# Both halves of the key's low part: a score matmul over 128 rows instead of 64

## The chip, the cores and the metric

The kernel runs on one core of one Trainium2 chip. The metric is device microseconds of one execution; three runs of the kernel before gave a median of 2198.81 us (2196.29 to 2199.24). Times inside a profile are microseconds from the start of its span.

## The reference, cut to what matters

One inference step of a one-layer decoder: 2048 prompt positions behind 16 meta tokens, and 8 sample positions, 1024 channels. Queries have 8 heads of 64, keys and values 2 heads of 64; every query sees itself and the 128 positions before it.

```python
h = rmsnorm(x); p = h @ w_in          # q 8x64 | k 2x64 | v 2x64 | conv GLU a 512 | b 512
s = einsum('...qhgd,...khd->...hgqk', q, k) * HEAD_DIM ** -0.5   # scores, per KV head h, group g
s = where(valid, s + rel_bias, -inf); softmax with a sink per head; o = p @ v
c = swish(layernorm(depthwise_conv_31(a * sigmoid(b))))
x = x + concat(o, c) @ w_out
x = x + square(relu(rmsnorm(x) @ w_up)) @ w_down;  y = rmsnorm(x)
```

## The kernel before

All matmuls run in a reduced 32-bit format (`F32R`), and full precision is put together from parts: each operand is split into a high part (a cast on ScalarE) and a low part (a subtraction on VectorE), and high x high, high x low and low x high are added up in PSUM. A weight slab of 128 output channels so costs 24 matmuls (`pe_step`, line 210): 8 blocks of 128 input channels times three.

The tokens are cut into five tiles (`PT`, line 25: 384, 448, 448, 448 and 320 prompt positions). Tile 0 also carries the 16 meta tokens (400 columns) and the last tile the 8 samples (328). For each tile the program (`prog`, line 943) runs the input projection (14 slabs), attention and convolution, the output projection (8 slabs) and the feed-forward part (64 slabs). Attention and convolution of a tile run as generators in the background (`Background`, line 46): after each slab of matmuls they are given a budget of VectorE time. The last slabs of tile 0's input projection share their weights with tile 1 (`in2`). The order in which each engine issues its instructions is fixed when the program is built, by a scheduler that simulates the engines and takes the ready instruction of highest priority; on the chip every engine works through its own list in order.

The score part of attention. When the slab of K has been computed (`win_evac_scaled`, m == 8, line 440), K lies on 128 partitions: KV head 0 on 0 to 63, KV head 1 on 64 to 127. For each KV head `kv`, the high part is written to both partition halves of `kh[kv]` by two casts (lines 449, 450), and the low part, one subtraction (line 451), to the head's own half of `kl`, which the two heads share. A query head's tile `q` (lines 486 to 489) holds the high part of q in the head's own half and the low part in the other half. So `q` against `kh[kv]` over 128 rows gives high x high and low x high at once, and a second matmul over the 64 rows of the own half adds high x low. These two are lines 544 and 545 in `attn_gen`. It loops over query blocks (`BQ`: 3 blocks of 128 in tile 0, 4 of 112 in tiles 1 to 3, 4 of 80 in tile 4) and over KV heads; per block and KV head it issues one group of 8 score matmuls, for 4 query heads two each, with 240 columns for blocks of 112, 208 for blocks of 80, and 256 or 144 in tile 0. In the profile the 128-row ones read `128*112 128x240` and the 64-row ones `64*112 64x240` (rows * columns of the weights, then the moving operand). In all there are 19 blocks x 8 heads = 152 pairs, of which 24 are in tile 0.

The scores of a group go to two PSUM tiles `s`; VectorE adds the bias and takes the maximum (line 558), ScalarE exponentiates and scales, TensorE transposes (`pt`, line 577), ScalarE and VectorE split the result (`ph`, `pl`), and TensorE multiplies it with V (`st`).

What else the change touches: for tiles 1 to 4, `kk` holds the two high planes and the low plane of K (line 394), and the last 128 keys of a tile go to the next one through `khist` (lines 444 to 466). In tile 0 these are single slots of the pool `tp`, 52 slots (`NSLOT`, line 1067) that also hold the input x, the normalized input's high and low parts (16 slots a tile), the queries, the convolution's inputs and sums (`pre`, line 709) and the diagonal weights of the convolution channel that TensorE computes (`dgs`, line 826; its matmuls are `cps`). `bias_setup` (line 919) spreads the relative-position bias through DRAM (`scr`, `bias`), issued from GpSimd.

Of the kernel before, what the change touches and what calls it, by code (L numbers as in the profile page):

```python
# [8 lines left out]
F32R = mybir.dt.float32r  # L9
AF = mybir.ActivationFunctionType  # L10
ALU = mybir.AluOpType
# [21 lines left out]
TM = max(TI)  # L33
# [43 lines left out]
def trunk(tc, x_in, w_all, smalls, rel, ck, cv, sconv, y_out, kv_out, ck_out, cv_out, up_out, us_out):  # L77
    nc = tc.nc
    with ExitStack() as ctx:
# [4 lines left out]
        at = ctx.enter_context(tc.tile_pool(name="at", bufs=1))  # L84
# [19 lines left out]
        def dcost(ap, extra=0.0):  # L104
            n = 1
            for s in ap.shape[1:]:
                n *= s
            clock[0] += n / 960.0 + 0.07 + extra

        def tt(out, a, b, op):  # L110
            dcost(out)
            return nc.vector.tensor_tensor(out, a, b, op=op)  # L112
# [21 lines left out]
        def cpy(out, a):  # L134
            return nc.scalar.copy(out, a)  # L135

        def f(ap):
            return ap.bitcast(F32)

        def slot(dt=F32):  # L140
            t = tp.tile([128, TS], dt, tag="t", name="t")
            return t
# [12 lines left out]
        def mm(out, lhsT, rhs, start, stop):  # L155
            return nc.tensor.matmul(out, lhsT, rhs, start=start, stop=stop)  # L156
# [222 lines left out]
        def win_alloc(i):  # L379
            n = TI[i]  # L380
            s = st[i]
            if i == 0:
                k0 = slot(F32R)
                k1 = slot(F32R)
                kl = slot(F32R)
                vt = slot()
                s["kh"], s["kl"], s["vt"], s["ko"] = [k0[:, :n], k1[:, :n]], kl[:, :n], vt[:, :n], 0
                s["u"] = []
                for c in range(4):
                    t = slot()  # L390
                    nc.vector.memset(t[:, :CW - 1], 0.0)
                    s["u"].append(t[:, :CW - 1 + n])
            else:
                kk = at.tile([128, 3, 128 + TM], F32R, tag="kk", name="kk")
                vt = at.tile([128, 128 + TM], F32, tag="vt", name="vt")
                s["kh"], s["kl"], s["vt"], s["ko"] = [kk[:, 0], kk[:, 1]], kk[:, 2], vt[:, :], 128
                s["kk"] = kk
                u = at.tile([128, 4, CW - 1 + TM], F32, tag="u", name="u")
                s["u"] = [u[:, c, :] for c in range(4)]
            s["q"] = {}  # L400
# [14 lines left out]
        def win_evac_scaled(i, m):  # L415
            n = TI[i]
            s = st[i]
            last = i == NT - 1
            if m < 8:
                c = m // 2  # L420
                if m % 2 == 0:
                    def ev(ps):
                        sg = tmp()
                        act(sg[:, :n], ps[:, :n], AF.Sigmoid)
                        s["sg"] = sg
                else:
                    def ev(ps):
                        u = s["u"][c]
                        if i > 0:
                            cpy(u[:, :CW - 1], st[i - 1]["uh"][:, c, :])  # L430
                        tt(u[:, CW - 1:CW - 1 + n], ps[:, :n], s["sg"][:, :n], ALU.mult)
                        if "uh" not in s:
                            uh = at.tile([128, 4, CW - 1], F32, tag="uh", name="uh", bufs=2)
                            s["uh"] = uh
                        e = CW - 1 + OFF[i] + PT[i]
                        cpy(s["uh"][:, c, :], u[:, e - (CW - 1):e])
                        s.setdefault("udone", []).append(c)
                        if c == 3 and last:
                            nc.gpsimd.dma_start(up_out, s["uh"])
            elif m == 8:  # L440
                def ev(ps):
                    o = s["ko"]
                    if i > 0:
                        p = st[i - 1]["khist"]
                        cpy(s["kk"][:, :, :128], f(p))
                    for kv in range(2):
                        hr, xr = HR[kv], HR[1 - kv]
                        kh = s["kh"][kv][:, o:o + n]
                        cpy(kh[hr], ps[hr, :n])
                        cpy(kh[xr], ps[hr, :n])  # L450
                        tt(s["kl"][hr, o:o + n], ps[hr, :n], f(kh[hr]), ALU.subtract)
                    e = o + OFF[i] + PT[i]
                    if last:
                        e0 = OFF[i] + PT[i]
                        kvo = at.tile([128, 2, 128 + NSMP], F32, tag="kvo", name="kvo")
                        s["kvo"] = kvo
                        cpy(kvo[:, 0, :], ps[:, e0 - 128:e0 + NSMP])
                    else:
                        kn = at.tile([128, 3, 128], F32R, tag="khist", name="khist")
                        if i > 0:  # L460
                            cpy(kn, f(s["kk"][:, :, e - 128:e]))
                        else:
                            cpy(kn[:, 0, :], f(s["kh"][0][:, e - 128:e]))
                            cpy(kn[:, 1, :], f(s["kh"][1][:, e - 128:e]))
                            cpy(kn[:, 2, :], f(s["kl"][:, e - 128:e]))
                        s["khist"] = kn
            elif m == 9:
                def ev(ps):
                    o = s["ko"]
                    if i > 0:  # L470
                        cpy(s["vt"][:, :128], st[i - 1]["vhist"])
                    cpy(s["vt"][:, o:o + n], ps[:, :n])
                    e = o + OFF[i] + PT[i]
                    if last:
                        cpy(s["kvo"][:, 1, :], s["vt"][:, e - 128:e + NSMP])
                        nc.gpsimd.dma_start(kv_out, s["kvo"])
                    else:
                        vn = at.tile([128, 128], F32, tag="vhist", name="vhist")
                        cpy(vn, s["vt"][:, e - 128:e])
                        s["vhist"] = vn  # L480
            else:
                def ev(ps):
                    c = m - 10
                    for kv in range(2):
                        hr, xr = HR[kv], HR[1 - kv]
                        q = slot(F32R)
                        s["q"][kv * 4 + c] = q
                        act(q[hr, :n], ps[hr, :n], AF.Copy, scale=HD ** -0.5)
                        stt(q[xr, :n], ps[hr, :n], HD ** -0.5, f(q[hr, :n]), ALU.mult, ALU.subtract)
                    if last:  # L490
                        if c == 0:
                            qs = at.tile([128, NSMP, NH], F32, tag="qs", name="qs")
                            nc.vector.memset(qs, 0.0)
                            s["qs"] = qs
                        e = OFF[i] + PT[i]
                        for kv in range(2):
                            r = HR[kv]
                            act(s["qs"][r, :, kv * 4 + c], ps[r, e:e + NSMP], AF.Copy, scale=HD ** -0.5)
            return ev
# [14 lines left out]
        def attn_gen(i, blocks):  # L514
            s = st[i]
            bq = BQ[i]
            for b in blocks:
                q0 = b * bq
                qc = OFF[i] + q0
                kc = s["ko"] + qc  # L520
                k0 = max(kc - 128, 0)
                na = kc - k0
                nk = na + bq
# [11 lines left out]
                for kv in range(2):  # L535
                    hr, xr = HR[kv], HR[1 - kv]
                    sp = []
                    for c in range(4):
                        if c % 2 == 0:
                            t = pa.tile([128, 2, 256], F32, tag="s", name="s")  # L540
                            sp.append(t)
                        o = sp[-1][:bq, c % 2, :nk]
                        q = s["q"][kv * 4 + c]
                        mm(o, q[:, qc:qc + bq], s["kh"][kv][:, k0:k0 + nk], True, False)
                        mm(o, q[hr, qc:qc + bq], s["kl"][hr, k0:k0 + nk], False, True)
                    if i > 0 or NS0 == 1:
                        yield STEP
                    p = at.tile([128, 4, 256], F32, tag="p", name="p", bufs=NPB)
# [43 lines left out]
                    o = ot[:, :4 * bq]  # L592
# [575 lines left out]
def build(shapes):  # L1168
    import concourse.bacc as bacc

    nc = bacc.Bacc("TRN2", target_bir_lowering=False, num_devices=1)
    args = [nc.dram_tensor(n, s, F32, kind="ExternalInput").ap() for n, s in shapes.items()]
    args += [nc.dram_tensor(n, s, F32, kind="ExternalOutput").ap() for n, s in _OUTS]
    with tile.TileContext(nc, schedule_with_timeline_sim=True) as tc:
        trunk(tc, *args)
    return nc
# [28 lines left out]
```

## Time and profile before

| | |
|---|---|
| median of 3 runs | 2198.81 us |
| span of the profiled execution | 2192.0 us |
| median less span | 6.8 us |
| TensorE matmul busy | 2143.6 us (98%) |
| TensorE weight loads busy | 1976.0 us (90%) |
| VectorE busy | 1520.4 us (69%) |
| ScalarE busy | 1178.2 us (54%) |

The profiled execution's own time outside its span is not given, so the span stands for it. TensorE's 48.4 us without a matmul lie in four places: the first 20 us, the stretch from 50 to 97 us, short waits up to 360 us, and the last 92 us. Matmuls are pipelined: the duration of one is not the time it takes from the next, so costs of matmuls are read here from start to start.

### The profile page before, as it was taken

Reading aid. Unit: us, or ns where it says so; the run is one execution under the profiler, and the core shown is the slowest. Engines: PE = TensorE matmul, PEld = TensorE weight load, DVE = VectorE, ACT = ScalarE, POOL = GpSimd, SP = SyncE. Lnnn points to the kernel's source line nnn. Section 1 sums busy time; section 2 is a strip of 40 time slices with the busy share of each in tenths; the row PEclk is TensorE's granted clock in tenths of the full one; section 3 lists DMA queues with packets and bytes.
Section 4 is the critical chain, followed back from the end, with each engine's and each line's share of the span. In section 5 each row is a group of like instructions: output and inputs, shape, how many; then the busy total and the mean of one; then the engine's idle time right before and its main releaser. Section 6 shows DMA issues by size and latency. Waiting matters only on the chain.

```text
span 2192.0 us, 29953 instructions
## 1 busy us (share of the span) xinstructions
PE 2143.6 (98%) x11330; PEld 1976.0 (90%) x11330; DVE 1520.4 (69%) x2585; ACT 1178.2 (54%) x2151; POOL 50.0 (2%) x95
## 2 busy tenths in 40 slices
PE   7599999999999999999999999999999999999998
PEld 6587899999998898989989898899998989999998
DVE  5497698986866987647758886466787754565444
ACT  6357475467545454655445447454654464454443
POOL 1000000000000000000000000000010100000000
PEclk9799999999999999999999999999999999999999
DMA  5311323324433222225332222335432322435442
GB/s 186 68 49 54 130 91 121 116 106 139 162 132 105 98 87 97 97 98 171 140 108 94 96 96 87 106 121 183 148 106 100 126 90 103 150 117 187 145 152 103
DMA packets 77952, 255.67 MB, mean 117 GB/s; under 512 B 9805, under 2 KB 20173, under 8 KB 77808
## 3 DMA queue, kind: packets, MB, share of 16 engines
q1 hardware_dynamic: 72000, 238.08, 31.5%
q0 software_dynamic: 5088, 14.93, 2.4%
q8 instruction: 89, 1.46, 0.3%
q10 hardware_dynamic: 720, 0.76, 0.1%
q14 instruction: 55, 0.45, 0.1%
HBM read 241.97 MB, written 11.75 MB: 116 GB/s over the span
## 4 chain that ended last, share of the span: by engine, by line
PE 95%; issue 2%; DMA 2%; DVE 1%; POOL 0%; ACT 0%; DVEq 0%; POOLq 0%; ACTq 0%
PE mm L156 87%; PE s L156 4%; PE st L156 2%; DMA scr<-t 2%; PE pt L577 1%; PE cps L156 1%; DVE t L116 0%; DMA bias<-scr 0%; DMA t<-x_in 0%; DVE wlo L112 0%; PE mx L156 0%; PE st L525 0%; PE st L526 0%; DVE t L112 0%; DVE m L116 0%
## 5 line engine op out<-in xcount | busy, mean ns | idle before, releaser
L156 PE MATMUL mm<-t,whi 128*128 128x448 f32 (+3 forms) x6560 | 1354.2, 353 | 12.4 <-ACT t L131 8.7
L156 PEld LDWEIGHTS mm<-t,whi 128*128 128x128 f32 x6560 | 1168.8, 189 | 86.7 <-ACT t L131 9.5
L135 ACT CAST whi<-raw 128x1024 fp32r<-128x1024 f32 x424 | 443.7, 1049 | 599.0 <-PE mm L156 485.4
L156 PE MATMUL mm<-t,wlo 128*128 128x448 f32 (+3 forms) x3280 | 714.0, 350 | 0.0
L112 DVE TENSOR_TENSOR wlo<-raw,whi 128x1024 fp32r<-128x1024 f32 x424 | 516.7, 1219 | 262.5 <-PE mm L156 140.1
L156 PEld LDWEIGHTS mm<-t,wlo 128*128 128x128 f32 x3280 | 588.8, 188 | 34.0
L116 DVE SCALAR_TENSOR_TENSOR t<-u,sm,t 128x448 f32<-128x448 f32 (+1 forms) x480 | 300.8, 645 | 3.5
L112 DVE TENSOR_TENSOR t<-mm,t 128x448 f32<-128x448 f32 (+2 forms) x200 | 116.6, 583 | 209.7 <-PE mm L156 206.7
L112 DVE TENSOR_TENSOR t<-m,t 128x448 fp32r<-128x448 f32 (+3 forms) x234 | 133.1, 581 | 25.6 <-ACT t L135 24.9
L135 ACT CAST t<-m 128x448 fp32r<-128x448 f32 (+3 forms) x236 | 125.3, 536 | 17.5 <-DVE m L116 12.8
L131 ACT ACTIVATE m<-mm 128x448 f32<-128x448 f32 (+2 forms) x176 | 90.0, 511 | 56.8 <-PE mm L156 49.3
L131 ACT ACTIVATE m<-t 128x448 f32<-128x448 f32 (+3 forms) x140 | 72.1, 542 | 65.0 <-DVE t L112 42.1
L132 ACT ACTIVATE p<-p,nm 112x240 f32<-112x240 f32 (+3 forms) x152 | 72.2, 476 | 49.0 <-DVE nm L121 48.7
L131 ACT ACTIVATE m<-m 128x448 f32<-128x448 f32 (+3 forms) x164 | 90.1, 549 | 3.9
L558 DVE CUSTOM_DVE_ANT_0 p<-s,bias,sm 112x240 f32<-112x240 f32 (+3 forms) x152 | 61.7, 449 | 30.8 <-DMA bias<-scr 25.7
L156 PE MATMUL s<-kk,t 128*112 128x240 f32 (+3 forms) x256 | 72.4, 341 | 1.7 <-DVE t L116 1.7
L156 PEld LDWEIGHTS s<-kk,t 128*112 128x112 f32 (+3 forms) x256 | 42.2, 165 | 32.0 <-issue 8.2
L131 ACT ACTIVATE p<-p,rd 112x240 f32<-112x240 f32 (+3 forms) x152 | 62.0, 476 | 9.9 <-DVE rd L127 9.7
L112 DVE TENSOR_TENSOR ss<-ss,m 128x448 f32<-128x448 f32 (+3 forms) x100 | 58.3, 583 | 6.9 <-ACT m L131 3.6
L127 DVE RECIPROCAL rs<-m 128x448 f32<-128x448 f32 (+2 forms) x15 | 41.6, 2776 | 24.1 <-ACT m L131 24.1
L116 DVE SCALAR_TENSOR_TENSOR t<-t,sm 128x384 f32<-128x384 f32 (+1 forms) x98 | 56.6, 612 | 2.4 <-ACT t L131 2.0
L156 PE MATMUL mm<-cah,whi 128*128 128x448 f32 (+2 forms) x160 | 55.6, 349 | 1.6 <-ACT cah L135 0.7
(174 smaller groups left out, 1144.8 us busy)
## 6 DMA issues: line engine op xcount, KB each, us to landing
raw<-w_all SPq DMA_DIRECT2D x424, 512.0 KB, 3.2
t<-x_in SPq DMA_DIRECT2D x40, 224.0 KB, 5.0
y_out<-t POOLq DMA_DIRECT2D x24, 224.0 KB, 3.4
t<-x_in SPq DMA_DIRECT2D x16, 164.0 KB, 3.6
t<-x_in POOLq DMA_DIRECT2D x8, 224.0 KB, 6.3
t<-x_in SPq DMA_DIRECT2D x8, 200.0 KB, 5.1
scr<-t POOLq DMA_DIRECT2D x1, 1536.0 KB, 33.2
t<-x_in SPq DMA_DIRECT2D x8, 192.0 KB, 5.1
```

Source lines behind the costliest of these rows:

```text
L112: return nc.vector.tensor_tensor(out, a, b, op=op)
L116: return nc.vector.scalar_tensor_tensor(out, a, s, b, op0=op0, op1=op1)
L127: return nc.vector.reciprocal(out, a)
L131: return nc.scalar.activation(out, a, f, bias=bias, scale=scale)
L132: return nc.scalar.activation(out, a, f, bias=bias, scale=scale, accum_out=accum_out)
L135: return nc.scalar.copy(out, a)
L156: return nc.tensor.matmul(out, lhsT, rhs, start=start, stop=stop)
L558: nc.vector.tensor_tensor_reduce(out=p[:bq, c, :nk], in0=sp[c // 2][:bq, c % 2, :nk], in1=bias[:bq, h, b0:b0 + nk], scale=1.0, scalar=sm[: ...
L577: nc.tensor.transpose(t[:r, c * bq:(c + 1) * bq], p[:bq, c, a:a + r], idn[:bq, :bq])
```

## The change

The low part of K gets a plane of its own for each KV head, written into both partition halves, and the second score matmul then runs over all 128 rows, with the same weights `q` as the first. (Its other half now multiplies the query's low part with the key's low part, a product that was not formed before.) Per tile this adds two subtractions; `kk` and `khist` get a fourth plane; tile 0 uses one slot of `tp` more. The on-chip memory that is set aside for the descriptors of GpSimd's DMAs is halved, to 8192 bytes a partition.

```diff
@@ win_alloc @@
-                kl = slot(F32R)
+                l0 = slot(F32R)
+                l1 = slot(F32R)
...
-                kk = at.tile([128, 3, 128 + TM], F32R, tag="kk", name="kk")
+                kk = at.tile([128, 4, 128 + TM], F32R, tag="kk", name="kk")
...
@@ win_evac_scaled, m == 8 @@
-                        tt(s["kl"][hr, o:o + n], ps[hr, :n], f(kh[hr]), ALU.subtract)
+                        kl = s["kl"][kv][:, o:o + n]
+                        tt(kl[hr], ps[hr, :n], f(kh[hr]), ALU.subtract)
+                        tt(kl[xr], ps[hr, :n], f(kh[hr]), ALU.subtract)
...
-                        kn = at.tile([128, 3, 128], F32R, tag="khist", name="khist")
+                        kn = at.tile([128, 4, 128], F32R, tag="khist", name="khist")
...
@@ attn_gen @@
                         mm(o, q[:, qc:qc + bq], s["kh"][kv][:, k0:k0 + nk], True, False)
-                        mm(o, q[hr, qc:qc + bq], s["kl"][hr, k0:k0 + nk], False, True)
+                        mm(o, q[:, qc:qc + bq], s["kl"][kv][:, k0:k0 + nk], False, True)
...
@@ build @@
-    nc = bacc.Bacc("TRN2", target_bir_lowering=False, num_devices=1)
+    nc = bacc.Bacc("TRN2", target_bir_lowering=False, num_devices=1, dynamic_dma_scratch_size=8192)
```

## Rows read from the trace of the kernel before

**Rows 1.** The page: busy time of each engine, and the chain that ended last.
```profile
PE 2143.6 (98%) x11330; PEld 1976.0 (90%) x11330; DVE 1520.4 (69%) x2585; ACT 1178.2 (54%) x2151; POOL 50.0 (2%) x95
...
PE 95%; issue 2%; DMA 2%; DVE 1%; POOL 0%; ACT 0%; DVEq 0%; POOLq 0%; ACTq 0%
```

**Rows 2.** Stretches: length, busy time (instructions) of each engine, granted clock, DMA share, GB/s.
```profile
150.00:216.00 66.00, 64.92 (x282) 49.01 (x281) 53.20 (x117) 47.48 (x114) 0.00 (x0) 1.00 0.11 40
...
251.00:690.00 439.00, 436.98 (x2376) 415.62 (x2376) 340.58 (x564) 249.93 (x455) 4.30 (x8) 1.00 0.35 122
690.00:1148.00 458.00, 458.00 (x2249) 413.20 (x2247) 324.93 (x527) 241.63 (x426) 4.32 (x8) 1.00 0.32 111
```

**Rows 3.** Groups by shape: count, busy us, mean ns, idle before: the 64-row score matmuls.
```profile
L156 PE MATMUL s<-kk,t 64*112 64x240 f32 x96 | 34.8, 362 | 0.0
...
L156 PE MATMUL s<-kk,t 64*80 64x208 f32 x32 | 10.2, 320 | 0.0
...
L156 PE MATMUL s<-t 64*128 64x256 f32 x16 | 6.1, 381 | 0.0
```

**Rows 4.** Timeline, one group of 8 score matmuls: start, length, engine, what, count.
```profile
370.93 2.32 PE L156 MATMUL s<-kk,t 128*112 128x240 f32 x8
...
371.13 1.93 PEld L156 LDWEIGHTS s<-kk,t 64*112 64x112 f32 x7 [0.20 <-issue]
...
373.18 0.45 PE L156 MATMUL mm<-t,whi 128*128 128x384 f32 x1
```

**Rows 5.** Timeline of TensorE: groups of other widths, and the matmul that follows each.
```profile
162.43 2.46 PE L156 MATMUL s<-t 128*128 128x256 f32 x8
164.82 4.14 PE L156 MATMUL cps<-t 128*128 128x384 f32 x12
...
1584.75 2.02 PE L156 MATMUL s<-kk,t 128*80 128x208 f32 x8
1586.70 1.29 PE L156 MATMUL mm<-t,whi 128*128 128x448 f32 x5
```

**Rows 6.** Timeline of TensorE: series without a change of rows, and what follows each.
```profile
385.78 0.93 PE L577 MATMUL pt<-idn,p 112*128 112x112 f32 x8
386.48 0.59 PE L156 MATMUL mm<-t,whi 128*128 128x384 f32 x2
...
1986.88 2.54 PE L156 MATMUL mm<-t,whi 128*128 128x328 f32 x16
1989.25 1.36 PE L156 MATMUL mm<-t,wlo 128*128 128x328 f32 x8
```

**Rows 7.** Timeline of TensorE: two matmuls over 112 rows, right behind ones over 128.
```profile
393.39 0.36 PE L156 MATMUL st<-ph,vv 112*128 112x448 f32 x1
393.59 0.36 PE L156 MATMUL st<-pl,vv 112*128 112x448 f32 x1
```

**Rows 8.** TensorE's waits: who for whom, total us, times, longest.
```profile
PE s L156 <- DVE mx L558: 21.8, 1, 21.8
```

**Rows 9.** Timeline of tile 0's convolution: VectorE, ScalarE and TensorE.
```profile
130.62 0.47 DVE L122 TENSOR_SCALAR t<-t,sm 128x384 f32<-128x384 f32 x1
...
182.43 5.17 DVE L116 SCALAR_TENSOR_TENSOR t<-t,sm 128x384 f32<-128x384 f32 x8
...
145.10 1.85 ACT L131 ACTIVATE t<-idn,sm 128x128 f32<-128x128 f32 x6
...
193.13 0.58 ACT L131 ACTIVATE t<-cps,sm 128x384 f32<-128x384 f32 x1 [2.43 <-PE cps L156]
...
215.15 0.44 PE L156 MATMUL mm<-cah,whi 128*128 128x384 f32 x1 [0.67 <-ACT cah L135]
```

**Rows 10.** The present subtractions of the low part, and GpSimd's DMA queue.
```profile
L112 DVE TENSOR_TENSOR kk<-mm,kk 64x448 fp32r<-64x448 f32 x6 | 3.7, 620 | 2.4 <-ACT kk L135 2.3
...
q0 software_dynamic: 5088, 14.93, 2.4%
...
bias<-scr POOLq DMA_DIRECT2D x1, 1024.0 KB, 6.1
```

More of the change, by code (lines that the diff above doesn't have):

```diff
@@ L384, in win_alloc @@
                 k1 = slot(F32R)
-                kl = slot(F32R)
+                l0 = slot(F32R)
+                l1 = slot(F32R)
                 vt = slot()
-                s["kh"], s["kl"], s["vt"], s["ko"] = [k0[:, :n], k1[:, :n]], kl[:, :n], vt[:, :n], 0
+                s["kh"], s["kl"], s["vt"], s["ko"] = [k0[:, :n], k1[:, :n]], [l0[:, :n], l1[:, :n]], vt[:, :n], 0
                 s["u"] = []
@@ L393, in win_alloc @@
             else:
-                kk = at.tile([128, 3, 128 + TM], F32R, tag="kk", name="kk")
+                kk = at.tile([128, 4, 128 + TM], F32R, tag="kk", name="kk")
                 vt = at.tile([128, 128 + TM], F32, tag="vt", name="vt")
-                s["kh"], s["kl"], s["vt"], s["ko"] = [kk[:, 0], kk[:, 1]], kk[:, 2], vt[:, :], 128
+                s["kh"], s["kl"], s["vt"], s["ko"] = [kk[:, 0], kk[:, 1]], [kk[:, 2], kk[:, 3]], vt[:, :], 128
                 s["kk"] = kk
@@ L464, in ev @@
                             cpy(kn[:, 1, :], f(s["kh"][1][:, e - 128:e]))
-                            cpy(kn[:, 2, :], f(s["kl"][:, e - 128:e]))
+                            cpy(kn[:, 2, :], f(s["kl"][0][:, e - 128:e]))
+                            cpy(kn[:, 3, :], f(s["kl"][1][:, e - 128:e]))
                         s["khist"] = kn
```

## The prediction, made before the changed kernel was run

> **What bounds the kernel now.** I read the page first: TensorE's matmuls fill 98% of the span, and the chain that ended last runs over TensorE for 95% of it [rows 1]. VectorE is next, at 69%. The reader is to see that everything except TensorE's list is cover, as long as it comes in time. The stretches say where: from 690 to 1148 us, TensorE is busy for 458.00 of 458.00 us at the full granted clock while VectorE has 324.93, and between 251 and 690 us for 436.98 of 439.00 with VectorE at 340.58 (78%) [rows 2]. A microsecond taken from TensorE's list there is a microsecond of the end. Tile 0 is another matter: the waits show one stall of 21.8 us in front of a score matmul [rows 8], before the position bias has come, and between 150 and 216 us VectorE is at 53.20 of 66.00 [rows 2] and the output projection begins on a wait [rows 9].
>
> A busy TensorE isn't one at its peak, so I went on to the timeline of one score group. Eight matmuls of 240 columns start at 370.93, and the next slab's matmul starts at 373.18: 2.25 us, 281 ns for each [rows 4]. A series without a change of rows goes much faster: 16 matmuls of 328 columns from 1986.88 to 1989.25 are 148 ns each [rows 6], and 448 columns 200 ns [rows 7], both 0.45 ns a column; 240 columns would be 108 ns. In the group the first weight load over 64 rows comes 0.20 us behind the start of the first matmul, with TensorE's load path idle and nothing named that it waited for [rows 4]; in a plain series the loads are ahead of their matmuls. So each step from 128 to 64 rows or back lets the matmul before run out and then loads in the open, some 170 ns on top. That it is the half array, and not merely fewer than 128 rows, is seen where 112-row weights follow 128-row ones: 393.39 to 393.59 is the plain 200 ns for 448 columns [rows 7].
>
> **The change on TensorE.** It removes no matmul and no column. It makes all eight of a group of one kind. New price of one: 0.45 ns a column, so 108 ns at 240 columns and 94 ns at 208. The trace of before has no series of 128-row, 112-wide weights with 240 columns; the bounds are 88 ns from below (112 by 112 transposes, 8 in the 0.70 us from 385.78 to 386.48) and 148 ns from above (the 328-column row) [rows 6]. I take 108, which is nearest in shape to the long series.
> - Tiles 1 to 3: 96 of the 64-row matmuls of 240 columns [rows 3], so 24 groups. Each goes from 2.25 us [rows 4] to 8 x 0.108 = 0.86 us: 1.39 us less. 24 x 1.39 = 33.3 us.
> - Tile 4: 32 of 208 columns [rows 3], 8 groups. Each goes from 1.95 us (1584.75 to 1586.70 [rows 5]) to 8 x 0.094 = 0.75: 1.20 less. 8 x 1.20 = 9.6 us.
> - Tile 0: 16 of 256 columns [rows 3], 4 groups, from 2.39 us (162.43 to 164.82 [rows 5]) to 8 x 0.115 = 0.92: 4 x 1.47 = 5.9 us. Its two groups of 144 columns I put at 1.1 each, between nothing and 1.47: 2.2 us. Together 8.1 us.
>
> The first two lie on TensorE where it has no idle time, and count in full, except that between 251 and 360 us it already waits about 2 us (439.00 less 436.98 [rows 2]) and may wait a little more when it comes earlier: I take 1 us off. That is 41.9 us.
>
> **Tile 0 keeps little of its 8.1 us.** Three of its pairs or so lie before the stall of 21.8 us [rows 8] and only lengthen it. The rest lie between 96 and 176 us, ahead of the join at 215.15 us, where the output projection waits 0.67 us for the attention's last piece, just behind the convolution's norm [rows 9]. TensorE's list gets there 7 us sooner; VectorE's does not, and it has a new handicap. Count the slots of `tp` while attention 0 runs: normalized inputs of tiles 0 and 1, 32; K 3; V 1; queries 8; convolution inputs 4; the norm's scale 1. That is 49, and the first three sums `pre` make 52, the whole pool. The trace agrees: the first diagonal weights of `cps`, which need slot 53, are written at 145.10 us [rows 9], when the last slab of tile 0 lets go of the first input. With one more slot for K the third sum must wait for that too. Today its first tap is at 130.62 and its last ends at 187.6 [rows 9]. It would begin at about 145 less the some 5 us that TensorE has gained by then, 10 us late; 8 taps take 5.17 us, so at most 15 taps, 10 us of VectorE work, are pushed behind. From 150 to 216 us VectorE has 12.8 us idle [rows 2] to take them up, and the last sum is in any case not wanted before `cps` is done at 193.1 us [rows 9]. So the norm begins between 4 us earlier and 6 us later than now: the 8.1 us come out between +7 (all kept) and -6. I take +0.5.
>
> **The rest.** Each tile has two subtractions more, 0.62 us each [rows 10]: 1.2 us on VectorE, 6 us in the kernel. They stand ahead of weight splits on VectorE's list, and TensorE works on slabs that were split one step (about 5 us) before; nothing to pay, and 6 us if that cover were gone. The fourth plane of `kk` and `khist` makes 7 ScalarE copies of 0.51 us a third longer, about 1 us in all, under the same cover. The smaller descriptor memory: no row shows a GpSimd DMA that waits for room. From below it costs nothing; from above, another landing like that of the bias, 6.1 us [rows 10], in the stall of tile 0, where it would move the end in full. All of GpSimd's queue is 5088 packets on 16 engines in 2192 us, 2.4% of their time [rows 10]; I take 0.
>
> **Sum.** 33.3 + 9.6 - 1.0 + 0.5 = 42.4 us. The profiled span is 2192.0, so 2149.6 after; the median of the runs stands 6.8 us over the span, and gives 2156. The order of each engine's list is made anew by a simulated schedule in which one slot and ten subtractions are different; I take 1 us for new small waits: 2157 us.
>
> A rule speaks against all this. The Trainium skill, "TensorE: Matmul & The Clock Gate", sections "LDWEIGHTS (loading the stationary operand)" and "Why this matters for your kernels", has the cost of a load follow from its columns and says that a matmul over few rows takes the same time as one over 128. By it the two matmuls of a pair cost alike already and filling the rows saves nothing. The 0.20 us in front of the 64-row load and 281 against 108 ns [rows 4, 6] don't agree with that for a change of rows from one matmul to the next.
>
> **Rivals.**
> - *Nothing is gained*: the slow pace belongs not to the change of rows but to something the new pairs keep, such as adding up in one PSUM bank or reloading the same query weights. Then 2199 us, or 2201 with the new subtractions. Against it: series that add into one bank run at 148 ns [rows 6], and the 112-row weights pay nothing [rows 7]. For it: the trace has no such pair over 128 rows twice. This is also where the page's rule ends. 4%.
> - *Only part comes through* because VectorE or ScalarE become late: TensorE's list arrives earlier at transposes and weights that aren't ready. VectorE goes from 78% to 340.58 / (439.00 - 11) = 80% there [rows 2]. If every second group's gain were waited away, 21 us are left: 2178 us. 5%.
> - *Tile 0 pays for the slot*: the convolution's norm comes 6 us late and none of the 8.1 us stays, and a bit more is lost on a last tap: 2192.0 - 41.9 + 8 + 6.8 = 2165 us. For it: the full pool; against it: the 12.8 us of idle VectorE. 15%.
> - *Slower*: the slot that is missing is not a sum of the convolution but one of tile 1's normalized input. Then the slabs of tile 1 that share weights with tile 0 (6 slabs of 24 x 0.200 us [rows 7], 29 us) can't run until queries are let go, at the group of 162.43 [rows 5] at the earliest, and TensorE, which works through its list in order, stands for those 29 us and for as much of tile 0's other half as is queued behind, another 20: 42 less 49 is 7 us slower, 2206 us. It decides from a wait of 43 us on. Against it: the eight slots of tile 1's x come free one by one just as its parts are written, well before the sums take theirs. 4%.
>
> **How the numbers follow.** The forecast, 2157 us, has 72%. Its own range: 40 fewer nanoseconds saved on each of 256 matmuls in tiles 1 to 4 is 10 us up (2167), 6 us of tile 0 up again (2173); 20 ns more saved on each is 5 us down and 7 us of tile 0 kept 7 down (2145). A landing of 6.1 us for the smaller descriptor memory would stand in the place of tile 0's 6, in the same stall or just behind it. The third rival lies inside. So 2145 to 2174. About 0.2% is what a measurement of this kernel can tell from no change: faster 92%, the same 4%, slower 4%.
>
> **What would show it.** Right: score groups of 8 in 0.8 to 1.0 us for 240 columns, from their first start to the next slab's; no idle load path in front of every second one; TensorE's matmuls at 98% or more of a span near 2150; the stretch from 251 us to the end of tile 4's attention some 42 us shorter. The slot: the third sum's first tap behind the first diagonal weights, and a longer wait at the first output matmul of tile 0. Wrong: groups still above 1.5 us, or new waits of TensorE for `p`, `wlo` or a slot that add up to more than 5 us.

## The result

| | before | after |
|---|---|---|
| median of the runs | 2198.53 us (2196.29 to 2199.24) | 2149.33 us (2148.80 to 2150.56) |
| span of the profiled execution | 2192.0 us | 2147.7 us |
| TensorE matmul busy | 2143.6 us | 2093.9 us |
| VectorE busy | 1520.4 us | 1524.6 us |

The ratio of after to before is 0.9784 (95% interval 0.9770 to 0.9798): 49 us less by the medians, 44.3 us less by the two spans. The forecast was 2157 us, between 2145 and 2174.

The page of after, busy times and the chain, as in [rows 1]:

```profile
PE 2093.9 (97%) x11330; PEld 1963.9 (91%) x11330; DVE 1524.6 (71%) x2595; ACT 1178.0 (55%) x2152; POOL 50.2 (2%) x95
...
PE 94%; issue 2%; DMA 2%; DVE 1%; POOL 0%; ACT 0%; DVEq 0%; POOLq 0%; ACTq 0%
```

The same number of matmuls takes 49.7 us less of TensorE, VectorE has ten instructions and 4.2 us more, and the chain runs over TensorE as before.

The timeline of after, a group of 240 columns with what follows, and one of 208 (start, length, engine, what, count); it answers to [rows 4] and [rows 5]:

```profile
367.31 1.00 PEld L156 LDWEIGHTS s<-kk,t 128*112 128x112 f32 x8
367.48 1.04 PE L156 MATMUL s<-kk,t 128*112 128x240 f32 x8
...
368.36 1.38 PE L156 MATMUL mm<-t,whi 128*128 128x384 f32 x7
...
1550.12 0.94 PE L156 MATMUL s<-kk,t 128*80 128x208 f32 x8
1550.89 1.39 PE L156 MATMUL mm<-t,whi 128*128 128x448 f32 x6
```

Eight matmuls from 367.48 to 368.36 are 110 ns each, where they were 281; the weight loads run ahead of them as one series (the first at 367.31), and the line `[0.20 <-issue]` of [rows 4] is gone. With 208 columns they are 96 ns, from 1550.12 to 1550.89.

Stretches of after from tile 1 on, cut at about the same places as in [rows 2] (length, busy of TensorE, its loads, VectorE, ScalarE, GpSimd; granted clock):

```profile
246.00:685.00 439.00, 436.48 (x2438) 421.87 (x2437) 348.95 (x585) 254.32 (x461) 4.32 (x8) 1.00 0.36 125
685.00:1136.00 451.00, 451.00 (x2274) 414.79 (x2274) 329.77 (x535) 247.29 (x441) 4.34 (x8) 1.00 0.33 114
```

TensorE stays full: 451.00 of 451.00 us. VectorE rises to 348.95 of 439.00 (79%, from 78%) and takes almost nothing back: TensorE is without a matmul for 2.52 us of the first stretch, against 2.02 in [rows 2].

Where tile 0 ends: the first 448-column slab behind tile 0's output projection, before and then after.

```profile
251.68 3.42 PE L156 MATMUL mm<-t,whi 128*128 128x448 f32 x16
```

```profile
251.83 3.42 PE L156 MATMUL mm<-t,whi 128*128 128x448 f32 x16
```

By these marks nothing is gained up to here, and all 44.4 us (1940.3 us from this place to the end of the span, against 1895.9) come behind it. The two executions already differ before the scores begin: the first score matmul behind the stall of 21.8 us starts at 96.18 us before and at 97.40 after. Counted from it, tile 0 takes 155.5 us before and 154.4 after, so that 1.1 us are gained. Lines of tile 0 of after, on VectorE, ScalarE and TensorE, answer to [rows 9]:

```profile
142.48 0.47 DVE L122 TENSOR_SCALAR t<-t,sm 128x384 f32<-128x384 f32 x1
...
141.47 0.99 ACT L131 ACTIVATE t<-idn,sm 128x128 f32<-128x128 f32 x3 [0.18 <-PE mm L156]
...
205.09 0.83 PE L156 MATMUL mx<-ones,ss 128*128 128x1 f32 x6 [3.48 <-DVE ss L112]
...
212.26 0.42 PE L156 MATMUL mm<-cah,whi 128*128 128x384 f32 x1
...
218.16 0.48 PE L156 MATMUL s<-kk,t 128*112 128x240 f32 x2 [2.27 <-DVE t L116]
```

The convolution's third sum begins at 142.48, behind the first diagonal weights, instead of at 130.62. TensorE's waits (who for whom; total, times, longest) show two that the kernel before doesn't have in this size:

```profile
PE s L156 <- DVE t L116: 4.1, 3, 2.3
PE mx L156 <- DVE ss L112: 3.5, 1, 3.5
```

The second is new: TensorE stands 3.5 us, up to 205.09, for the sum of squares of the convolution's norm. The first was 1.7 us before; its 2.27 us at 218.16 lie behind the first matmul of the output projection. That matmul still comes 2.9 us sooner than before (212.26 against 215.15), and the lead is lost by the mark at 251.83. The granted clock falls behind both waits, as two stretches of after show (same columns as above):

```profile
204.00:218.00 14.00, 10.80 (x52) 9.88 (x52) 6.78 (x12) 8.53 (x14) 0.00 (x0) 0.88 0.14 48
218.00:232.00 14.00, 13.21 (x65) 12.54 (x66) 8.07 (x14) 5.47 (x10) 0.00 (x0) 0.88 0.51 178
```

The kernel before has 1.00 in both. A mean of 0.88 means that part of each stretch ran at the lower level of the clock, 1.2 instead of 2.4 GHz; it is 12% of 28 us, an estimate of 3.4 us lost.

### The profile page after: what moved, and what is told of

Read it like the earlier page. It is cut to its first block, busy times and chain, and to the rows that moved or that the text cites. A ratio compares the mean times of both kernels' runs of the same rounds, so it can differ in the third digit from the quotient of the medians.

```text
span 2147.7 us, 29970 instructions
## 1 busy us (share of the span) xinstructions
PE 2093.9 (97%) x11330; PEld 1963.9 (91%) x11330; DVE 1524.6 (71%) x2595; ACT 1178.0 (55%) x2152; POOL 50.2 (2%) x95
## 4 chain that ended last, share of the span: by engine, by line
PE 94%; issue 2%; DMA 2%; DVE 1%; POOL 0%; ACT 0%; DVEq 0%; POOLq 0%; ACTq 0%
PE mm L156 88%; PE st L156 2%; DMA scr<-t 2%; PE s L156 1%; PE pt L581 1%; PE cps L156 1%; DVE t L116 0%; DMA bias<-scr 0%; DMA t<-x_in 0%; DVE t L112 0%; DVE wlo L112 0%; DVE m L116 0%; PE mx L156 0%; DVE ss L112 0%; PE st L529 0%
## 5 line engine op out<-in xcount | busy, mean ns | idle before, releaser
L156 PE MATMUL mm<-cal,whi 128*128 128x448 f32 (+2 forms) x160 | 56.0, 352 | 0.0
L920 POOL DMA_DIRECT2D y_out<-t x32 | 17.3, 544 | 1609.6 <-DVE t L116 1607.7
```

Source lines behind the costliest of these rows:

```text
L920: q.dma_start(y_out[:, YO[i] + c * n:YO[i] + (c + 1) * n], y[:, :n])
```

## The experiments

The theory was that each change between 128 and 64 rows costs TensorE time, and that tile 0's share of the gain is eaten by the slot that K's second low plane takes. The rivals were that the gain comes from elsewhere (addresses, the descriptor memory, another order of the lists), that a 64-row matmul is slow by itself, and that tile 0 loses by the added subtractions.

**Undoing the matmul alone** (`e1_half_rows_back`), on the changed kernel:

```diff
-                        mm(o, q[:, qc:qc + bq], s["kl"][kv][:, k0:k0 + nk], False, True)
+                        mm(o, q[hr, qc:qc + bq], s["kl"][kv][hr, k0:k0 + nk], False, True)
```

> The changed kernel with all its planes, slots and descriptor memory, but the second score matmul over 64 rows again. Theory (each change between 128 and 64 rows costs about 0.17 us of TensorE): groups of 8 score matmuls of 240 columns back at 2.2 to 2.3 us, and the time back at 2194 to 2201 us. Rival (the gain came from elsewhere: another order of the lists, other addresses, the smaller descriptor memory): the time stays within 5 us of the changed kernel, 2145 to 2155 us. If the part that stood beyond the sum (about 4 us of pace in the other matmuls) belongs to addresses, 2193 to 2196.

Measured: 2205.17 us (2202.66 to 2206.09), ratio to before 1.0027 (1.0015 to 1.0039). Its timeline, a group, the loads, and the mark at which tile 0 ends:

```profile
379.67 2.31 PE L156 MATMUL s<-kk,t 128*112 128x240 f32 x8
381.92 1.83 PE L156 MATMUL mm<-t,whi 128*128 128x384 f32 x9
...
379.87 1.92 PEld L156 LDWEIGHTS s<-kk,t 64*112 64x112 f32 x7 [0.20 <-issue]
...
260.31 3.42 PE L156 MATMUL mm<-t,whi 128*128 128x448 f32 x16
1593.65 2.02 PE L156 MATMUL s<-kk,t 128*80 128x208 f32 x8
```

The group is back at 2.25 us with the same 0.20 us in front of the first 64-row load. So the whole gain hangs on the rows of this one matmul. More than that: everything else that the change brings makes the kernel 8.0 us slower than before by the medians, and the time lies 4 us over the expected 2194 to 2201. Almost all of the delay lies in tile 0: 260.31 against 251.68 is 8.6 us (with the first score matmul behind the stall at 96.24, against 96.18), and at the first group of tile 4 it is still 8.9 us (1593.65 against 1584.75 [rows 5]).

**The descriptor memory alone** (`e2_scratch_alone`), on the kernel before:

```diff
-    nc = bacc.Bacc("TRN2", target_bir_lowering=False, num_devices=1)
+    nc = bacc.Bacc("TRN2", target_bir_lowering=False, num_devices=1, dynamic_dma_scratch_size=8192)
```

> The kernel before with the smaller descriptor memory alone, which also moves every tile to other addresses. Theory: no effect, 2196 to 2200 us, in the same order of the lists. Rival: the some 4 us that the matmuls outside the score groups gained, or the 5 us by which the medians fell more than the spans, come from it: 2193 to 2195 us. A loss of up to 6 us if a GpSimd DMA has to wait for room.

Measured: 2198.83 us (2192.66 to 2199.50), ratio 1.0001 (0.9992 to 1.0010). Neither the smaller memory nor the addresses that move with it are worth anything beyond 0.1%.

**Fewer changes of rows with the same 64-row matmuls** (`e4_sorted`), on the kernel before; the flags that open and close a sum follow, since two heads share a bank:

```diff
-                        mm(o, q[:, qc:qc + bq], s["kh"][kv][:, k0:k0 + nk], True, False)
-                        mm(o, q[hr, qc:qc + bq], s["kl"][hr, k0:k0 + nk], False, True)
+                        mm(o, q[:, qc:qc + bq], s["kh"][kv][:, k0:k0 + nk], c % 2 == 0, False)
+                    for c in range(4):
+                        o = sp[c // 2][:bq, c % 2, :nk]
+                        q = s["q"][kv * 4 + c]
+                        mm(o, q[hr, qc:qc + bq], s["kl"][hr, k0:k0 + nk], False, c % 2 == 1)
```

> The kernel before, but the four 128-row matmuls of a group are issued first and the four 64-row ones behind them, so that a group has two changes of rows instead of eight. Nothing else moves; K keeps its one low plane. Theory (the change of rows costs): 6 x 0.17 = 1.04 us less for each group of 240 columns, 6 x 0.15 = 0.9 for 208, 24 x 1.04 + 8 x 0.9 = 32 us in tiles 1 to 4, little of tile 0: 2164 to 2170 us. Rival (a 64-row matmul is slow by itself, whatever its neighbours): the groups stay at 2.2 us and the time at 2196 to 2200 us.

Measured: 2158.17 us (2157.21 to 2158.59), ratio 0.9816 (0.9801 to 0.9831). A group in its timeline:

```profile
398.81 1.22 PE L156 MATMUL s<-kk,t 128*112 128x240 f32 x8
...
399.96 0.65 PEld L156 LDWEIGHTS mm<-t,whi 128*128 128x128 f32 x4
399.96 0.79 PE L156 MATMUL mm<-t,whi 128*128 128x384 f32 x3
```

Four matmuls over 128 rows and four over 64 take 1.15 us, against 2.25 when they alternate and 0.88 when all are over 128. A 64-row matmul is thus not slow by itself. The six changes of rows that went took 1.10 us, 0.18 us each. The two that remain cost as much. They take 0.27 us inside the group and some 0.10 us more on the first slab matmuls behind it, whose first load is not ahead: three of them take 0.79 us, and less the last one's 0.34 that is 0.45 us for two steps, against 0.35 us at the pace of 0.174 us for each that the slab has in after. Together that is 0.37 us, 0.18 to 0.19 each.

The time is 6 us under the expected 2164 to 2170 us. In tiles 1 to 4 the expected 32 us came out: 24 x 1.10 and 8 x 0.93 are 34 us, and from the first 448-column slab (here at 248.85) to the end the profiled execution is 33.2 us shorter than before. Tile 0 ends 2.8 us sooner. The other 3 of the 39 us stand between the medians alone; the profiled execution of before was a quick one (below).

**Leaving the second matmul out** (`e5_no_low`), on the changed kernel; the low part of K is missing from the scores:

```diff
-                        mm(o, q[:, qc:qc + bq], s["kh"][kv][:, k0:k0 + nk], True, False)
-                        mm(o, q[:, qc:qc + bq], s["kl"][kv][:, k0:k0 + nk], False, True)
+                        mm(o, q[:, qc:qc + bq], s["kh"][kv][:, k0:k0 + nk], True, True)
```

> The changed kernel without the second score matmul: the low part of K is left out of the scores. It measures what the now uniform second matmul still costs, and whether TensorE's time in the groups still counts one to one. Theory: 96 x 0.111 + 32 x 0.097 = 13.8 us less in tiles 1 to 4, 2134 to 2138 us. Rival (VectorE or ScalarE have become the bound in the attention stretches): 2145 to 2150 us.

Measured: 2134.53 us (2133.62 to 2136.91), ratio 0.9713 (0.9697 to 0.9729). That is 14.8 us less than the changed kernel by the medians. In tiles 1 to 4, where 13.8 us were expected, the profiled executions differ by 12.7 us (from the mark, here at 248.72, to the end: 1883.2 us against 1895.9), and by 3.1 us up to the mark. TensorE's time still counts nearly one to one there, and this is all that the uniform second matmul costs; its 64-row form cost 57 us in that place (1940.3 less 1883.2).

**The slot** was tested from four sides, each with one line, the length of the pool:

```diff
-NSLOT = 52
+NSLOT = 53
```

It is 53 in `e6_slots53` and, on top of the half rows of `e1_half_rows_back`, in `e7_half_rows53`; 55 in `e3_slots55`; and 51 in `e8_before_slots51`, which is the kernel before with nothing else changed.

> The changed kernel with 53 slots, just the one that the second low plane takes. Theory: as with 55 for the third sum, which is the one that waited; the diagonal weights still wait, as in the kernel before: 2141 to 2147 us. Rival: 2148 to 2151 us.

> The changed kernel with 55 slots in the pool instead of 52; the memory taken from the descriptors has room for them. Theory (tile 0 lost its gain to the slot that K's second low plane takes): the convolution's third sum starts near 126 us instead of 142.5, the diagonal weights no later, the output projection of tile 0 is reached 4 to 9 us sooner, and the time is 2140 to 2146 us. Rival (the two subtractions or the join itself eat tile 0's gain): 2148 to 2151 us.

> The changed kernel with the second score matmul over 64 rows again (which took 2205 us) and 53 slots. Theory (the 8 us over the kernel before are the missing slot): back at the kernel before, 2194 to 2200 us, with the third sum's first tap near 130 us. Rival (they are the added subtractions and wider copies): 2203 to 2207 us.

> The kernel before with 51 slots and nothing else. Theory (one slot is worth 8 us in tile 0): 2203 to 2208 us, third sum's first tap near 146 us, and from tile 0's output projection on a constant distance of some 8 us to the kernel before. Rival (the slot is harmless): 2195 to 2200 us.

The last column counts from the first score matmul behind the stall, since executions differ by up to 3.5 us in when they reach it.

| run | slots | time | ratio to before | first 448-column slab behind tile 0 | from the first score matmul behind the stall |
|---|---|---|---|---|---|
| kernel before | 52 | 2198.53 us | 1 | 251.68 us | 155.5 us (from 96.18) |
| changed kernel | 52 | 2149.33 us | 0.9784 | 251.83 us | 154.4 us (from 97.40) |
| `e6_slots53` | 53 | 2143.52 us | 0.9752 (0.9738 to 0.9767) | 243.83 us | 147.7 us (from 96.18) |
| `e3_slots55` | 55 | 2143.28 us | 0.9752 (0.9738 to 0.9767) | 245.92 us | 147.2 us (from 98.74) |
| `e1_half_rows_back` | 52 | 2205.17 us | 1.0027 | 260.31 us | 164.1 us (from 96.24) |
| `e7_half_rows53` | 53 | 2197.58 us | 1.0000 (0.9991 to 1.0009) | 256.08 us | 156.4 us (from 99.68) |
| `e8_before_slots51` | 51 | 2218.50 us | 1.0093 (1.0077 to 1.0110) | 261.99 us | 162.5 us (from 99.52) |

With one slot more, the third sum begins at its old place in the list and the output projection of tile 0 is reached 5.1 us earlier still (timeline of `e6_slots53`; compare the lines of after above):

```profile
126.97 0.47 DVE L122 TENSOR_SCALAR t<-t,sm 128x384 f32<-128x384 f32 x1
...
207.19 0.42 PE L156 MATMUL mm<-cah,whi 128*128 128x384 f32 x1
...
243.83 3.42 PE L156 MATMUL mm<-t,whi 128*128 128x448 f32 x16
```

Tile 0 then keeps 7.9 us of the forecast 8.1 (251.68 less 243.83, with the same start at 96.18). Against the changed kernel the slot is worth 6.8 us by the last column: TensorE is without a matmul for 2.8 us between 150 and 251 us, against 6.4, and the granted clock is 1.00 in the two stretches where it was 0.88, so that waits of 3.6 us and the clock's 3.4 us share the price about evenly. Three slots instead of one (55) change nothing more, although the diagonal weights are now written at 128.07 instead of 140.24: that wait was hidden.

The half rows with 53 slots are the kernel before again, to a tenth of a per cent, with the two subtractions and the wider copies still in: these cost nothing that shows.

The kernel before with 51 slots shows the slot without any of the change: the third sum at 149.17 us, behind the diagonal weights at 148.17. It is 20 us slower instead of the 8 expected: tile 0 takes 7 us more, and later tiles suffer too. In tile 2, three score groups come together with two transposes between them and no slab, and the last 16 matmuls run at 385 instead of 281 ns, as the timeline of `e8_before_slots51` shows (839.08 to 845.24):

```profile
836.64 2.31 PE L156 MATMUL s<-kk,t 128*112 128x240 f32 x8
...
839.08 6.23 PE L156 MATMUL s<-kk,t 128*112 128x240 f32 x16
845.24 0.74 PE L156 MATMUL mm<-t,whi 128*128 128x448 f32 x1
```

The stretch of these 16, in the same columns as the stretches of after (the granted clock is the third number from the end), and the four stretches behind tile 0, one a tile, where that clock is low:

```profile
839.08:845.30 6.22, 6.22 (x19) 3.48 (x17) 6.10 (x25) 3.24 (x13) 0.00 (x0) 0.69 0.00 0
...
282.00:302.00 20.00, 20.00 (x88) 16.79 (x88) 16.14 (x41) 11.74 (x29) 0.00 (x0) 0.84 0.10 40
842.00:862.00 20.00, 20.00 (x83) 16.96 (x83) 17.45 (x35) 11.93 (x31) 0.00 (x0) 0.84 0.33 106
1302.00:1322.00 20.00, 19.99 (x82) 17.09 (x82) 18.76 (x39) 12.38 (x31) 0.00 (x0) 0.83 0.32 105
1742.00:1762.00 20.00, 16.65 (x65) 13.13 (x65) 15.05 (x43) 13.96 (x42) 0.55 (x1) 0.66 0.21 65
```

The clock that these four lack is 20 x (0.16 + 0.16 + 0.17 + 0.34) = 16.6 us, an estimate; the kernel before lacks 1.9 us behind tile 0 (0.96 between 251.68 and 300). Behind the mark the two spans differ by 15.1 us (1955.4 against 1940.3). So the loss of the later tiles is lost clock, for the most part.

`e6_slots53` and `e3_slots55` beat both kernels: 55 us under the kernel before, 6 under the changed one.

## Why the prediction was right, and where its terms were off

**The price of a matmul.** Forecast 108 and 94 ns; measured 110 and 96. From groups of 2.25 and 1.95 us to 0.88 and 0.77 us: 24 x 1.37 + 8 x 1.18 = 42.3 us, where 42.9 were forecast. That the changes of rows were the cause was argued from the 112-row weights; `e1_half_rows_back` and `e4_sorted` show it.

**One term was missing.** Behind mark 251.68 the two spans differ by 44.4 us, not 41.9. The group was priced up to the start of the next slab's first matmul, but that one pays as well. In the timeline of before, the first five matmuls behind the group:

```profile
373.18 1.14 PE L156 MATMUL mm<-t,whi 128*128 128x384 f32 x5
```

In after, seven take 1.38 us (368.36, above): less the last one's 0.34, that is 0.174 us from start to start. Five at that pace would be 4 x 0.174 + 0.34 = 1.04 us, against 1.14: 0.1 us were lost to a load that did not run ahead. For 32 groups that is 3 us. The granted clock adds up to 1.9 us: 0.96 between 251.68 and 300 us before, 1.00 after. The gap is 44.4 - 42.3 = 2.1 us. What stands against these terms is 0.5 us more without a matmul (2.52 us against 2.02) and that the sum prices all 32 groups as whole ones, while some stand broken into pairs, at the start of tile 1 above all; this was not added up.

**Tile 0.** The forecast kept 0.5 of 8.1 us, so it put the slot at 7.6 us; 1.1 us were kept, or -0.15 by the bare marks, and the third sum begins at 142.48. The slot measures 6.8 us by `e6_slots53` and 7.7 by `e1_half_rows_back` against `e7_half_rows53`, from the first score matmul behind the stall (5.8 and 7.6 by the medians). The count of slots found the mechanism. The size was the middle of a range of 13 us, and about half of it came by the granted clock, which has no term in the forecast, so that the closeness is partly luck. The sign that was named, a longer wait at the first output matmul, did not come: the long wait stands at the norm's sum of squares, 7 us ahead of that matmul.

**Nothing paid.** Subtractions, wider copies and descriptor memory were put at nothing; `e7_half_rows53` and `e2_scratch_alone` say the same, each within 0.1%.

**The step from span to time was wrong.** I took 6.8 us between the profiled span and the median as what lies around the span. In every run whose span and time are both known they differ by 1.7 to 1.8 us (after: 2149.5 and 2147.7). The profiled execution of before was a quick one, some 2193.8 us, and the kernel before spreads over 2192.6 to 2199.9 us. So the 2149.6 forecast for the span met 2147.7, and 5 of the 8 us between 2157 and 2149 are this step. Part of the spread is there before any score matmul and has nothing to do with the change: between 17 and 31 us TensorE is busy for 13.6 us or more of the 14, but issues 74 matmuls in the profile of before, 62 in that of after, 72 in `e6_slots53` and 56 in `e7_half_rows53`, whose span of 2198.1 us is 6.1 over before; 3.5 of these are there at the first score matmul behind the stall. The runs also differ in their mean clock: 0.992 in the two quickest of the kernel before and of `e2_scratch_alone` (2192.64 and 2192.66 us), 0.988 in the slowest of both (2199.85 and 2199.50). Whether the changed kernel spreads less, its four runs don't tell.

**The rivals.** "Nothing is gained" falls with the groups' 0.88 us, "only part comes through" with TensorE's 451.00 of 451.00. "Tile 0 pays for the slot" was nearly the case: the slot's price took almost all of the 8.1 us, but no more. "Slower" by a missing slot of tile 1's input did not come; `e8_before_slots51` shows that a pool one slot shorter does make this kernel slower, by another way.

**The rule of the Trainium skill.** By "TensorE: Matmul & The Clock Gate" of the Trainium skill (section "LDWEIGHTS (loading the stationary operand)") a load costs by its columns, whatever its rows. The loads of this case agree: in the kernel before, those of 112 columns take 170 ns over 64 rows and 173 over 128 (means of 96 each). What decided this case is the change from one kind to the other. "TensorEngine Tiling (Array Packing)" of the Trainium skill, section "Tiling Modes", says that a change of tiling mode drains TensorE, and lists 64 rows as a mode of its own. If a 64-row matmul among 128-row ones is such a change, which no run here shows directly, the runs agree, at 0.18 to 0.19 us for each change.

## What to carry to other kernels

Where a matmul over half the rows stands among full ones, price it from start to start, with the load line beside it: an idle load path in front of it that nothing released was here the price of the change, and making both of one kind brought all of it back, sorting them most of it. An edit that takes one more buffer from a full pool needs a count of who holds the buffers at that moment, and of what then waits. A distance between one profile's span and a median may be the spread of the executions and not an overhead: compare span with span, stretches of two profiles from an event that both have, and look at the granted clock behind every new wait.

## What was not expected of the hardware

In `e8_before_slots51` the granted clock fell although TensorE was never without a matmul. It fell within a series of twenty-four score matmuls that alternate between 128 and 64 rows, with two transposes but no slab between them: its mean is 0.69 of full in 839.08 to 845.30, so part of the stretch ran at the lower of the two levels, 1.2 instead of 2.4 GHz, while the load path was busy for 3.48 of 6.22 us. The same series stands in tile 3 (from 1297.17), and there the mean is 0.83 in 1302 to 1322. A third series of twenty-four, in tile 4 (from 1738.42), has waits of TensorE in it, and 1742 to 1762 has 0.66. In all other runs no more than one group of eight stands between two slabs from 340 us on, and their clock is 1.00 up to 2060 us. That the alternation is the cause is argued from these places; no run tests it alone.
